# A SwiGLU whose turned results are copied out of their banks at the head of a gate group and split at its end

## The chip, the core and the metric

The kernel runs on one core of a Trainium2 chip. The metric is the device time of one execution in microseconds (us), the median of several runs; the profile is of one execution.

The engines are PE (matmul, with its weight load PEld), DVE (elementwise work on tensors), ACT (activations, copies and casts), POOL and SP (here they mostly issue DMAs). Results of PE land in PSUM, in eight banks of 128 x 512 float32; the other tiles lie in SBUF.

## What is computed

One layer of a decoder with 256 rows and a width of 2048: a combined projection, two kinds of attention, an output projection, a SwiGLU of inner width 5632 and a gated per-layer embedding, all in float32. What matters here is the SwiGLU:

```
f = rmsnorm(h, ffn_norm[i])
h = h + (jax.nn.silu(f @ w_gate[i]) * (f @ w_up[i])) @ w_down[i]
```

## The kernel before, in words

**Three products for one.** PE multiplies in a reduced float32 (type fp32r). To keep the precision, every operand is split in a high part (a cast to fp32r) and a low part (what the cast left out), and each product is made of three matmuls: high by high (line 400), the low part of the activations by the high part of the weights (401), and the high part of the activations by the low part of the weights (402). For each piece of a weight, ACT casts the high part (L352) from a raw tile that SP's DMA has filled, and DVE subtracts it from the raw tile to get the low part (L363). The parts lie in tiles called ringh and ringl, moreh and morel, and most. Some gate and up units are done by Strassen's scheme with seven products instead of eight: for those DVE also makes sums of the raw quarters (L362, L365, L366), and ACT and DVE hand pieces to each other.

**The order of the SwiGLU.** The inner width is cut in chunks of 1024 (the last has 512). The groups follow each other as g0, u0, g1, the first half of the down product of the chunk before, u1, its second half, g2 and so on. I call the down product that follows gate g1 "d1", and its halves the first and the second. The last chunk is one group for gate and up, gu5, and after it comes the last down product. Each group runs over units (one or two slices of 128 of the contracted dimension), and each unit over turns. In a turn, Python code emits casts and low parts of coming weights, then lets waiting side tasks do one step (`step`; a task says how many steps it wants to wait), then emits the matmuls. The engines take their instructions in the order in which they are emitted.

**The product that is turned.** When an up group ends, DVE multiplies its result with the silu of the gate into a tile called stage (L1012). The next group needs it turned, as the left operand of the down product: `ff_transpose` lets PE transpose it by blocks of 128 x 128 into four banks (L1032), four blocks in each, and `split_psum` makes the two parts from each bank: ACT casts the high part (L121) into ffTh, DVE subtracts (L122) into ffTl. All of this is emitted after the first product of the next gate group. The down product that reads ffTh and ffTl comes only after that gate group.

**What shares a tile.** Stage is one buffer. The end of a gate group (`gate_add`) takes it again: ACT copies the four gate banks into it (L997), POOL's DMA adds the Strassen sums U to it (L999), ACT applies silu (L1003), and the up group's end multiplies into it (L1012). Other work at these places: at the end of the Strassen units ACT copies a bank into U (L467) and DVE forms the sums there from the others (L468 to L471), which sets these banks free for the down product; at the end of a first down half ACT copies its four banks out (`add_later`, L915), and the up group that follows uses the same banks.

Of the kernel before, what the change touches and what calls it, by code (L numbers as in the profile page):

```python
# [8 lines left out]
F32 = mybir.dt.float32  # L9
# [4 lines left out]
ALU = mybir.AluOpType  # L14
# [21 lines left out]
def kernel(ctx, tc, x, p, positions, attn_norm, w_in, kv_norm, w_ukv, w_o, ffn_norm,  # L36
                             w_gate, w_up, w_down, ple_norm, w_ple_gate, w_ple_proj, final_norm,
                             inv_freq, out):
    nc = tc.nc
# [13 lines left out]
    def obank():  # L53
        b = B["rot"][B["next"] % len(B["rot"])]
        B["next"] += 1
        return b
# [62 lines left out]
    def split_psum(hi, lo, ps, scale=None):  # L119
        if scale is None:  # L120
            nc.scalar.copy(hi, ps)  # L121
            nc.vector.tensor_tensor(lo, ps, hi.bitcast(F32), op=ALU.subtract)  # L122
        else:
            nc.scalar.mul(hi, ps, scale)  # L124
            nc.vector.scalar_tensor_tensor(lo, ps, scale, hi.bitcast(F32), op0=ALU.mult, op1=ALU.subtract)
# [380 lines left out]
    def add(gen, wait=0, front=False):  # L506
        tasks.insert(0 if front else len(tasks), [wait, gen])
# [277 lines left out]
    def parts_tile(name, slot, shape=(8, SEQ)):  # L785
        return [big.tile([128, *shape], F32R, name=name + s, tag=f"{slot}{s}") for s in "hl"]
# [220 lines left out]
    def up_evac(ci, n, nb):  # L1007
        left = {"n": nb}

        def f(c, t, c0, c1, b, off=0):  # L1010
            st = S["ff"][:, t, c0 - off:c1 - off]
            nc.vector.scalar_tensor_tensor(st, b, S["rf"][:, t:t + 1], st, op0=ALU.mult, op1=ALU.mult)  # L1012
            left["n"] -= 1
            if left["n"] == 0:
                turned = ff_transpose(ci, n, S.pop("ff"))
                if ci < 5:
                    S["turned"] = turned
                else:
                    add(turned, 2)
        return f  # L1020

    def ff_transpose(ci, n, st):
        if ci == 5:
            ft = big.tile([128, 2, 6, SEQ], F32R, name="ffT", tag="att")
            tl = ffT[ci] = [ft[:, 0], ft[:, 1]]
        else:
            tl = ffT[ci] = parts_tile("ffT", "f0")
        for k in range(0, n // 128, 2):
            b = obank()
            for i in range(2):  # L1030
                for t in range(NT):
                    nc.tensor.transpose(b[:, (2 * i + t) * 128:(2 * i + t + 1) * 128],  # L1032
                                        st[:, t, (k + i) * 128:(k + i + 1) * 128], ident)
            split_psum(tl[0][:, k:k + 2, :], tl[1][:, k:k + 2, :], b.rearrange("q (a s) -> q a s", a=2))
            if k % 4 == 2:
                yield 1

    def ff_l(k, t):
        ci, kk = divmod(k, 8)
        return lhs_of(ffT[ci])(kk, t)  # L1040
# [224 lines left out]
    for k in range(2):  # L1265
        b = obank()
# [133 lines left out]
```

## Time and profile before

| | us |
|---|---|
| median of 3 runs | 1188.38 |
| range of the runs | 1187.52 to 1189.03 |
| the profiled execution | 1187.67 |
| its span, first to last instruction | 1185.9 |

In rows of the profile, a group names line, engine, operation, out<-in by tile names, the shape and a count. In rows of the timeline the first number is the start in us from the span's start, the second how long the row lasted; equal instructions that follow each other are one row with a count. In square brackets stands how long the engine was idle before the row and what ended that. Matmuls overlap, and their ends are modelled. "PEclk" is the clock that was granted to PE, as a share of the full one.

### The profile page before, as it was taken

The page shows a single profiled execution, that of the slowest core. Times are in us where ns is not written, and L with a number is a line of the kernel's source. Part 1 is how long each engine was busy: PE and PEld are TensorE (multiplying, and loading weights), DVE is VectorE, ACT ScalarE, POOL GpSimd, SP SyncE. Part 2 cuts the span into 40 slices and gives each one's busy share as a digit, 9 for nine tenths or more (in the row PEclk, how much of TensorE's full clock was granted, in tenths as well). Part 3 has the DMA queues.
Part 4 walks back from the last instruction along what each step waited for, and adds up shares of the span by engine and source line. Part 5 has one row for each costly group of instructions (what it writes and reads, how often), then busy time and mean ns, then how long its engine had stood idle before and what let it go on. Part 6 is the DMA issues. An engine that isn't in the chain of part 4 may idle for free.

```text
span 1185.9 us, 14606 instructions
## 1 busy us (share of the span) xinstructions
PE 1172.7 (99%) x5480; PEld 980.7 (83%) x5480; DVE 948.1 (80%) x1119; ACT 710.9 (60%) x908; POOL 57.3 (5%) x78
## 2 busy tenths in 40 slices
PE   9999999999999999999999999999999999999996
PEld 7888888899888888778888888888888888888886
DVE  5675756866567679998999899989998999897474
ACT  6735755456556754667657675658475756465453
POOL 5310000000000000000000000000000000000000
PEclk9999999999999999999999999999999999999999
DMA  9886877765584776596968697778768795846631
GB/s 303 288 341 213 293 270 264 261 213 200 200 335 141 284 250 229 202 310 173 339 218 301 178 332 227 274 209 326 238 216 262 268 279 198 329 145 220 202 107 72
DMA packets 87223, 287.80 MB, mean 243 GB/s; under 512 B 5676, under 2 KB 10080, under 8 KB 82544
## 3 DMA queue, kind: packets, MB, share of 16 engines
q1 hardware_dynamic: 77824, 240.15, 56.7%
q0 software_dynamic: 9040, 46.19, 14.2%
q8 instruction: 43, 0.70, 0.2%
q10 hardware_dynamic: 288, 0.52, 0.1%
q14 instruction: 28, 0.23, 0.1%
HBM read 252.24 MB, written 26.21 MB: 235 GB/s over the span
## 4 chain that ended last, share of the span: by engine, by line
PE 97%; DVE 1%; issue 1%; ACT 0%; POOL 0%; DVEq 0%; POOLq 0%
PE bank L402 31%; PE bank L400 31%; PE bank L401 31%; PE bank L138 1%; PE bank L593 1%; PE bank L1032 1%; PE bank L714 1%; PE bank L622 1%; DVE ringl L363 0%; PE bank L616 0%; PE bank L596 0%; PE bank L623 0%; PE bank L113 0%; DVE most L363 0%; DVE morel L363 0%
## 5 line engine op out<-in xcount | busy, mean ns | idle before, releaser
L352 ACT CAST ringh<-raw 128x1024 fp32r<-128x1024 f32 (+4 forms) x307 | 372.0, 1249 | 272.5 <-PE bank L401 113.6
L363 DVE TENSOR_TENSOR ringl<-raw,ringh 128x1024 fp32r<-128x1024 f32 (+4 forms) x307 | 443.4, 1467 | 105.8 <-ACT ringh L352 103.7
L400 PE MATMUL bank<-ringh,aT 128*128 128x512 f32 (+3 forms) x713 | 274.8, 385 | 0.0
L402 PE MATMUL bank<-ringl,aT 128*128 128x512 f32 (+3 forms) x713 | 270.6, 380 | 0.1
L401 PE MATMUL bank<-ringh,aT 128*128 128x512 f32 (+3 forms) x713 | 270.1, 379 | 0.0
L402 PEld LDWEIGHTS bank<-ringl,aT 128*128 128x128 f32 x713 | 133.9, 188 | 25.5 <-DVE ringl L363 1.3
L400 PEld LDWEIGHTS bank<-ringh,aT 128*128 128x128 f32 x713 | 134.1, 188 | 23.5 <-ACT aT L124 0.3
L401 PEld LDWEIGHTS bank<-ringh,aT 128*128 128x128 f32 x713 | 134.1, 188 | 23.4
L352 ACT CAST moreh<-raw 128x1024 fp32r<-128x1024 f32 (+2 forms) x70 | 79.8, 1174 | 19.4 <-DVE raw L362 9.2
L363 DVE TENSOR_TENSOR morel<-raw,moreh 128x1024 fp32r<-128x1024 f32 (+2 forms) x66 | 85.5, 1316 | 1.7 <-ACT moreh L352 1.2
L400 PE MATMUL bank<-ringh,ffTh 128*128 128x512 f32 x204 | 79.4, 389 | 0.0
L352 ACT CAST most<-raw 128x1024 fp32r<-128x1024 f32 (+2 forms) x58 | 56.8, 1006 | 37.7 <-DVE raw L362 14.4
L401 PE MATMUL bank<-ringh,ffTl 128*128 128x512 f32 x204 | 79.4, 389 | 0.0
L402 PE MATMUL bank<-ringl,ffTh 128*128 128x512 f32 x204 | 79.4, 389 | 0.0
L363 DVE TENSOR_TENSOR most<-raw,most 128x1024 fp32r<-128x1024 f32 (+2 forms) x58 | 66.3, 1163 | 1.6 <-ACT most L352 1.5
L362 DVE TENSOR_TENSOR raw<-raw 128x1024 f32<-128x1024 f32 x51 | 62.5, 1225 | 1.7
L402 PEld LDWEIGHTS bank<-ringl,ffTh 128*128 128x128 f32 x204 | 38.3, 188 | 8.0
L400 PEld LDWEIGHTS bank<-ringh,ffTh 128*128 128x128 f32 x204 | 38.3, 188 | 7.9
L401 PEld LDWEIGHTS bank<-ringh,ffTl 128*128 128x128 f32 x204 | 38.3, 188 | 7.9
L366 DVE TENSOR_TENSOR raw<-raw 128x512 f32<-128x512 f32 x51 | 35.3, 692 | 1.8
L365 DVE TENSOR_TENSOR raw<-raw 128x512 f32<-128x512 f32 x51 | 34.9, 684 | 0.0
L400 PE MATMUL bank<-most,aT 128*128 128x512 f32 x88 | 34.6, 393 | 0.0
(353 smaller groups left out, 1961.1 us busy)
## 6 DMA issues: line engine op xcount, KB each, us to landing
raw<-in_w_down SPq DMA_DIRECT2D x44, 1024.0 KB, 7.3
raw<-in_w_gate SPq DMA_DIRECT2D x35, 1024.0 KB, 7.6
raw<-in_w_up SPq DMA_DIRECT2D x32, 1024.0 KB, 7.6
raw<-in_w_in SPq DMA_DIRECT2D x40, 512.0 KB, 4.9
raw<-in_w_o SPq DMA_DIRECT2D x16, 1024.0 KB, 5.9
raw<-in_w_ple_gate SPq DMA_DIRECT2D x16, 1024.0 KB, 5.1
raw<-in_w_in SPq DMA_DIRECT2D x8, 1024.0 KB, 5.3
wsums<-in_w_up POOLq DMA_DIRECT2D x8, 1024.0 KB, 7.2
```

Source lines behind the costliest of these rows:

```text
L138: nc.tensor.transpose(b[:, (2 * i + t) * 128:(2 * i + t + 1) * 128], part[:, t, i * 128:(i + 1) * 128], ident)
L352: nc.scalar.copy(h[:, :, c0:c1], r[:, :, c0:c1])
L362: tt(f[:, 0:2], f[:, 1:2].to_broadcast([128, 2, 512]), f[:, 0:4:3], op=ALU.subtract)
L363: tt(l[:, :, c0:c1], r[:, :, c0:c1], h[:, :, c0:c1].bitcast(F32), op=ALU.subtract)
L365: tt(f[:, 3], f[:, 3], f[:, 0], op=ALU.subtract)
L366: tt(f[:, 2], f[:, 2], f[:, 3], op=ALU.subtract)
L400: nc.tensor.matmul(b, xh, h, start=start, stop=False)
L401: nc.tensor.matmul(b, xl, h, start=False, stop=False)
L402: nc.tensor.matmul(b, xh, l, start=False, stop=stop)
L593: nc.tensor.matmul(s[:, c0:c0 + nk], qT[:, q * 128:(q + 1) * 128], kT[:, 0:nk], start=True, stop=qpe is None)
L622: nc.tensor.matmul(o[:, 0:256], v(0), pT[:, 0:256], start=True, stop=False)
L714: nc.tensor.transpose(b[:, (2 * i + t) * 128:(2 * i + t + 1) * 128], src[:, t, col(i0 + i):col(i0 + i) + 128], ident)
```

## The change

For chunks 0 to 4, ACT no longer casts from the banks. It copies each turned bank, in float32, back into the place of stage that was just turned (L1040 of the changed kernel); the transposes themselves and their place are the same. A new task, `both_parts`, waits six steps, then emits one cast from stage to ffTh (L1047) in each of four steps, and then the four low parts from stage and ffTh (L1050): one, one, and the last two together. `front=True` puts the task ahead of others; as it is counted down in steps, it comes to stand in the last Strassen units and the last unit of the gate group. Chunk 5 is split as before.

```
         for k in range(0, n // 128, 2):
             b = obank()
...
-            split_psum(tl[0][:, k:k + 2, :], tl[1][:, k:k + 2, :], b.rearrange("q (a s) -> q a s", a=2))
+            h, l, f = tl[0][:, k:k + 2, :], tl[1][:, k:k + 2, :], b.rearrange("q (a s) -> q a s", a=2)
+            if ci == 5:
+                split_psum(h, l, f)
+            else:
+                kept = st[:, :, k * 128:(k + 2) * 128]
+                nc.scalar.copy(kept, f)
+                lows.append((l, kept, h))
             if k % 4 == 2:
                 yield 1
+
+        def both_parts():
+            for _, kept, h in lows:
+                nc.scalar.copy(h, kept)
+                yield 1
+            for i, (l, kept, h) in enumerate(lows):
+                nc.vector.tensor_tensor(l, kept, h.bitcast(F32), op=ALU.subtract)
+                if i < 2:
+                    yield 1
+        if lows:
+            add(both_parts(), 6, True)
```

Where this puts the instructions, on the engines that wait or are waited for. The rows are in the order in which an engine takes them; a minus is a row of the kernel before, a plus one of the changed kernel, and the number in a name such as raw_2917 tells buffers apart.

DVE at the head of g1, between the product of u0 and the first weights of the gate group:

```order
 L430 TENSOR_TENSOR U<-U,bank_80 128x512
 L1012 SCALAR_TENSOR_TENSOR stage<-U,rf,stage 128x512
-L122 TENSOR_TENSOR ffTl<-bank_77,ffTh 128x512
-L122 TENSOR_TENSOR ffTl<-bank_78,ffTh 128x512
-L122 TENSOR_TENSOR ffTl<-bank_79,ffTh 128x512
-L122 TENSOR_TENSOR ffTl<-bank_80,ffTh 128x512
 L363 TENSOR_TENSOR ringl<-raw_2917,ringh 128x1024 x2
 L363 TENSOR_TENSOR ringl<-raw_2919,ringh 128x1024
```

The four low parts are gone from here. On ACT, at the same place, four copies (L1040) stand where the four casts (L121) stood.

DVE at the end of g1 in the kernel before, from the last weights of the gate group to the first of d1:

```order
L363 TENSOR_TENSOR ringl<-raw_114,ringh 128x2048
L468 TENSOR_TENSOR U<-U,bank_80 128x512
L469 TENSOR_TENSOR U<-U,bank_78 128x512
L470 TENSOR_TENSOR U<-U,bank_79 128x512
L471 TENSOR_TENSOR U<-U,bank_79 128x512
L363 TENSOR_TENSOR morel<-raw_2917,moreh 128x2048
L363 TENSOR_TENSOR most<-raw_2919,most 128x2048
```

And the same place in the changed kernel:

```order
L363 TENSOR_TENSOR ringl<-raw_114,ringh 128x2048
L1050 TENSOR_TENSOR ffTl<-stage,ffTh 128x512 x2
L468 TENSOR_TENSOR U<-U,bank_80 128x512
L469 TENSOR_TENSOR U<-U,bank_78 128x512
L470 TENSOR_TENSOR U<-U,bank_79 128x512
L471 TENSOR_TENSOR U<-U,bank_79 128x512
L363 TENSOR_TENSOR morel<-raw_2917,moreh 128x2048
L1050 TENSOR_TENSOR ffTl<-stage,ffTh 128x512 x2
L363 TENSOR_TENSOR most<-raw_2919,most 128x2048
```

Two low parts now stand ahead of the sums of U, and two behind the first weights of d1.

ACT at the end of g1, with the engines whose semaphores an instruction waits for:

```order
+L1047 CAST ffTh<-stage 128x512
 L352 CAST ringh<-raw_113 128x1024 [waits DMAHW4_49,PE_49,Activation_49]
 L352 CAST ringh<-raw_113 128x1024 [waits PE_49,Activation_49]
+L1047 CAST ffTh<-stage 128x512
 L352 CAST ringh<-raw_114 128x2048 [waits DMAHW5_49,PE_49,Activation_49]
+L1047 CAST ffTh<-stage 128x512
 L467 COPY U<-bank_77 128x512 [waits PE_49]
 L352 CAST moreh<-raw_2917 128x2048 [waits DMAHW6_49,PE_49,Activation_49]
 L352 CAST most<-raw_2919 128x2048 [waits DMAHW7_49,DVE_49,PE_49]
-L997 COPY stage<-bank_83 128x512 [waits PE_49]
+L997 COPY stage<-bank_83 128x512 [waits DVE_49,PE_49,Activation_49]
 L997 COPY stage<-bank_84 128x512 [waits PE_49]
```

Three of the four casts are seen here (the first stands one row further up, ahead of another ringh cast). The first copy into stage, L997, has a new wait: for DVE's last low part, since that reads the stage tile which L997 writes. PE's order, and those of POOL and SP, stay as they were.

More of the change, by code (lines that the diff above doesn't have):

```diff
@@ L1027, in ff_transpose @@
             tl = ffT[ci] = parts_tile("ffT", "f0")
+        lows = []
         for k in range(0, n // 128, 2):
```

## The prediction

> **What bounds the kernel now.** First the page.
>
> ```profile
> PE 1172.7 (99%) x5480; PEld 980.7 (83%) x5480; DVE 948.1 (80%) x1119; ACT 710.9 (60%) x908; POOL 57.3 (5%) x78
> ```
>
> PE is the bound: its span is shortened only by a wait of PE that goes, and lengthened by every new one. So next the waits of PE, and their places in its timeline. Apart from its first instruction PE has, over the whole run, only two waits for another engine that reach 0.8 us, both in g1, the first gate group with the moved step at its head:
>
> ```profile
> 495.96 0.50 PE L402 MATMUL bank<-ringl,sumsmore_sums 128*128 128x512 f32 x1 [0.85 <-DVE ringl L363]
> ```
> ```profile
> 506.70 0.50 PE L402 MATMUL bank<-most,sumsmore_sums 128*128 128x512 f32 x1 [0.92 <-DVE most L363]
> ```
>
> Each waits for a low part that DVE had not finished. As a rule a matmul starts 0.23 us after the one before it, while its row lasts 0.39:
>
> ```profile
> 510.02 0.39 PE L401 MATMUL bank<-ringh,aT 128*128 128x512 f32 x1
> 510.25 0.50 PE L402 MATMUL bank<-ringl,aT 128*128 128x512 f32 x1
> ```
>
> So the idle of 0.85 and 0.92, with the 0.16 that two rows usually overlap, makes about 1.0 us for each stall. The windows view then shows why: between g1's head and 510.2 DVE does not pause, and the same holds in d1 (columns: stretch, its length, busy us of PE, PEld, DVE, ACT, POOL, then clock, DMA).
>
> ```profile
> 477.40:510.20 32.80, 31.03 (x136) 24.85 (x134) 32.45 (x34) 21.82 (x24) 0.00 (x0) 1.00 0.63 223
> ...
> 519.70:535.40 15.70, 15.70 (x71) 13.02 (x70) 15.48 (x16) 6.76 (x9) 0.00 (x0) 1.00 0.89 295
> ```
>
> **The head of a gate group.** Four copies take the place of four casts on ACT (L121 becomes L1040), and four low parts leave DVE. What that is worth depends on who waits for whom at g1's head:
>
> ```profile
> 474.31 2.06 ACT L121 CAST ffTh<-bank 128x512 fp32r<-128x512 f32 x4 [10.85 <-PE bank L1032]
> 476.23 1.08 ACT L352 CAST ringh<-raw 128x1024 fp32r<-128x1024 f32 x1
> ```
> ```profile
> 474.93 2.48 DVE L122 TENSOR_TENSOR ffTl<-bank,ffTh 128x512 fp32r<-128x512 f32 x4 [1.13 <-ACT ffTh L121]
> 477.34 1.23 DVE L363 TENSOR_TENSOR ringl<-raw,ringh 128x1024 fp32r<-128x1024 f32 x1
> ```
>
> DVE's first weight, ringl, starts at 477.34; the ringh that it needs ends at 476.23 + 1.08 = 477.31. So DVE does not start late because of its 2.48 us of low parts: it is held by ACT, whose four instructions stay where they were. In the new order DVE idles through these 2.48 us and starts ringl at the same moment. Gain of the head: 0, at best 0.1 us (ACT's casts beside DVE's reading were 0.03 us longer than its mean of 1.05). The two stalls stay, since DVE is full from there to the second.
>
> **The tail of g1, and d1.** Here the four casts and four low parts return. No row of before has these instructions, but the form from an SBUF tile is there:
>
> ```profile
> L122 DVE TENSOR_TENSOR aT<-stage,aT 128x512 fp32r<-128x512 f32 x7 | 4.8, 691 | 13.2 <-ACT aT L121 13.2
> ```
> ```profile
> L121 ACT CAST aT<-stage 128x512 fp32r<-128x512 f32 x7 | 4.4, 622 | 0.2
> ```
>
> Instructions in a row overlap by some 0.08 us on DVE and 0.1 on ACT (four took 2.48 and 2.06), so each low part adds 0.61 us and each cast 0.52. The ends: at least the 0.60 and 0.49 of the rows from a bank; at most the full 0.69 and 0.62.
>
> The Trainium skill, "VectorE: DVE Perf Modes" (the section on the TRN2 errata), has another rule: a VectorE operation pays a smaller fixed cost from SBUF (58 cycles) than from PSUM (120), so a moved low part would be 0.06 us cheaper than before. The trace does not bear it out: 691 ns from SBUF here, 2.48 us for four from the bank. By that rule the sum below would be about 1.3 us lower (an estimate from the page: 0.26 us in each of five groups).
>
> Now ACT, DVE and PE at this place.
>
> ```profile
> 505.62 4.76 ACT L352 CAST ringh<-raw 128x1024 fp32r<-128x1024 f32 x4 [0.88 <-DVE raw L366]
> 510.29 0.57 ACT L467 COPY U<-bank 128x512 f32<-128x512 f32 x1
> 510.76 1.92 ACT L352 CAST moreh<-raw 128x2048 fp32r<-128x2048 f32 x1
> 512.57 1.91 ACT L352 CAST most<-raw 128x2048 fp32r<-128x2048 f32 x1
> 514.38 2.03 ACT L997 COPY stage<-bank 128x512 f32<-128x512 f32 x4
> 516.29 1.94 ACT L352 CAST ringh<-raw 128x2048 fp32r<-128x2048 f32 x1
> ```
> ```profile
> 507.85 2.35 DVE L363 TENSOR_TENSOR ringl<-raw,ringh 128x1024 fp32r<-128x1024 f32 x2
> 510.42 2.29 DVE L363 TENSOR_TENSOR ringl<-raw,ringh 128x2048 fp32r<-128x2048 f32 x1 [0.22 <-ACT ringh L352]
> ...
> 514.67 0.68 DVE L471 TENSOR_TENSOR U<-U,bank 128x512 f32<-128x512 f32 x1
> 515.26 2.28 DVE L363 TENSOR_TENSOR morel<-raw,moreh 128x2048 fp32r<-128x2048 f32 x1
> 517.47 2.28 DVE L363 TENSOR_TENSOR most<-raw,most 128x2048 fp32r<-128x2048 f32 x1
> 519.67 2.28 DVE L363 TENSOR_TENSOR ringl<-raw,ringh 128x2048 fp32r<-128x2048 f32 x1
> ```
> ```profile
> 517.41 0.39 PE L400 MATMUL bank<-ringh,ffTh 128*128 128x512 f32 x1
> ```
> ```profile
> 536.45 0.39 PE L400 MATMUL bank<-ringh,aT 128*128 128x512 f32 x1
> ```
>
> Step by step. (1) The first cast lies in ACT's 0.88 us of idle before 505.62, free. The second delays the ringh pair of 506.6 by 0.52, of which 0.2 was spare: DVE's two ringl end at 510.5 instead of 510.2, and PE, which took the second one 0.05 us after its end, at 510.25 (above), is 0.3 late. (2) With the third cast the big ringh ends at 510.38 + 1.04 = 511.42, DVE's big ringl starts 1.0 later. Two low parts behind it: L468 to L471 are 2.25 late, L471 ends at 517.6. PE takes its bank at 517.41 + 0.3 = 517.7: just covered; with the dearer ends above PE would lose up to 0.4 here. (3) morel, then the last two low parts: the last one ends at about 521.0.
>
> (4) Here is the new wait. L997 copies the new gate results into the one stage buffer, which now still holds the old results, so its first copy waits for the last low part: 521.05 instead of 514.38, 6.7 us. ACT takes its instructions in order, so behind it stand three more L997, POOL's DMA that adds U to that tile, nine casts of raw weights and then L915, which empties the banks of d1. The ringh cast runs at 522.96 and takes 1.94, so DVE's ringl of 519.67 starts at 524.95, 5.3 late. From there to 535.4 DVE has 0.2 us of slack in 15.7 (the window above), and ACT follows it piece by piece:
>
> ```profile
> 533.09 1.06 ACT L352 CAST most<-raw 128x1024 fp32r<-128x1024 f32 x1 [0.85 <-DVE raw L366]
> 534.05 0.57 ACT L915 COPY copied<-bank 128x512 f32<-128x512 f32 x1
> ```
>
> (5) L915 of bank 0 starts at 534.05 + 5.3 = 539.35 and ends at 539.92. PE's first matmul of u1 writes that bank; it wants it at 536.45 + 0.3 = 536.75 and gets it at 539.97: a stall of 3.2 us. g1 with d1: 3.5 us. Through u1 DVE then runs 0.6 us later against PE than before; I take that as covered, and as up to 0.3 us per group if not.
>
> Loads: the step issues no DMA. SP's loads into tiles that the late low parts release go out up to 5.3 us later; a tile is read again some 20 us after it is freed, so I cost that at 0.
>
> **The other groups.** g4 is placed as g1: L915 and the matmul behind it lie alike.
>
> ```profile
> 904.66 0.58 ACT L915 COPY copied<-bank 128x512 f32<-128x512 f32 x1
> ```
> ```profile
> 907.08 0.39 PE L400 MATMUL bank<-ringh,aT 128*128 128x512 f32 x1
> ```
>
> So 3.5 again. In g2 DVE is further ahead and pauses before L915:
>
> ```profile
> 640.81 2.29 DVE L363 TENSOR_TENSOR ringl<-raw,ringh 128x2048 fp32r<-128x2048 f32 x1 [0.46 <-ACT ringh L352]
> ```
> ```profile
> 654.92 1.22 DVE L363 TENSOR_TENSOR most<-raw,most 128x1024 fp32r<-128x1024 f32 x1 [0.77 <-ACT most L352]
> ```
> ```profile
> 656.06 0.59 ACT L915 COPY copied<-bank 128x512 f32<-128x512 f32 x1 [0.22 <-PE bank L402]
> ```
> ```profile
> 659.94 0.39 PE L400 MATMUL bank<-ringh,aT 128*128 128x512 f32 x1
> ```
>
> The ringl of 640.81 moves by 4.9 (the same wait), the pause takes up 0.8 to 0.9: L915 at 660.1, done at 660.7, PE wants bank 0 at 659.94: 0.8 us. g3 I take as g2. The last group, gu5, has no L997; there the DVE chain itself goes to the SwiGLU's last product (L1012), which PE turns next:
>
> ```profile
> 1017.55 0.75 DVE L1012 SCALAR_TENSOR_TENSOR stage<-U,rf,stage 128x512 f32<-128x512 f32 x1 [0.20 <-ACT stage L991]
> ```
> ```profile
> 1019.86 0.38 PE L1032 MATMUL bank<-ident,stage 128*128 128x128 f32 x2
> ```
>
> It ends at 1018.30 + 1.0 + 4 x 0.61 = 1021.8; PE's second turn, 0.1 after 1019.86 and 0.3 late, wanted it at 1020.3: 1.5, with the 0.3 of step (1) 1.8 us. Sum: 3.5 + 0.8 + 0.8 + 3.5 + 1.8 = 10.4 us. The profiled execution took 1187.67 (span 1185.9 and 1.8 around it), so 1198.1; it lies 0.7 under the median of 1188.38, so 1198.8 for the median.
>
> **The rivals.** *Only the near stalls* (slower, small): DVE or ACT makes up the 5.3 us before L915, and only 4 x 0.3 and gu5's 1.8 less 0.3 remain, 2.7 us: 1191.1. It needs 3.5 us of slack in 519.7 to 535.4, where the window shows 0.2. *Faster*: the 2.48 us taken from DVE's head let it start ringl early, both 1.0 us stalls and the three or so short ones of 0.1 at the gates' ends go, and the tail stays under cover: 1188.38 - 2.4 = 1186.0. For it speaks that DVE is full for 33 us after the head. It decides at the end of the first ringh: it would have to come about 2 us before 477.31, and the last low part before 517, not 521. *The clock*: a stall over 3 us might cost PE its rate. The run's first matmuls go at 0.42 us instead of 0.23:
>
> ```profile
> 5.04 1.69 PE L113 MATMUL bank<-junk 128*128 128x512 bf16 x4
> ```
>
> That lasted at least this row's 1.7 us and at most the 6.7 from the span's start to its end; half of it was lost, 0.8 to 3.4, in the middle 2.1. After each of the two stalls of 3.2 us that makes 4.2 more: 1203.0. Against it: the stalls of 1.0 us left the granted clock at 1.00. The Trainium skill, "TensorE: Matmul & The Clock Gate", Part 1, says that the clock halves after an idle window of about 3.4 us, which is just longer than the stall; no run here shows which.
>
> **How the numbers follow.** Forecast 0.76, near stalls only 0.09, clock 0.08, faster 0.05, and 0.02 that everything stays hidden at 1188. The forecast's own range: below, casts that fall into ACT's idle (0.5 in each of five groups, -2.5); above, the full durations (0.6 a group, +3.0) and 0.3 for each up group (+1.2): 1196.3 to 1203.0. The range reaches down for the case of near stalls in part and up into the clock's case: 1193.0 to 1203.5. A difference under 0.2%, 2.4 us, cannot be told from none. Faster by more than that 0.04, within it 0.07 (half of the near stalls' case, the rest of the faster one, the hidden one), slower 0.89.
>
> **What would show it.** Right: ringl at g1's head still starts with the end of ringh; the first L997 of g1 starts with the end of DVE's last L1050, about 6.7 us later against the gate's last matmul; PE waits for L915 at the heads of u1 and u4 for about 3 us, of u2 and u3 for under 1, and for L1012 in gu5. Wrong: the two stalls of g1 gone, or no wait of PE for L915.

## The result, and the profile after

The changed kernel takes 1202.54 us (median of 5 runs, 1200.41 to 1202.88), the kernel before 1188.38 us: a ratio of 1.0112, with a 95% interval of 1.0097 to 1.0126. It is slower, by 14.2 us where 10.4 were forecast; the time lies in the range of the prediction, near its upper end. The profiled execution took 1202.54 us, its span is 1200.8 us.

The engines' busy times on the page:

```profile
PE 1178.4 (98%) x5480; PEld 982.0 (82%) x5480; DVE 949.0 (79%) x1119; ACT 720.7 (60%) x928; POOL 55.8 (5%) x78
```

PE runs the same 5480 matmuls and is busy for 5.7 us more, in a span that is 14.9 us longer. The waits of PE (who waited for whom: us in total, times, the longest):

```profile
PE bank L400 <- ACT copied L915: 7.4, 4, 3.0
PE bank L113 <- DVE junk L108: 2.0, 1, 2.0
PE bank L1033 <- DVE stage L1012: 1.3, 1, 1.3
PE bank L402 <- DVE ringl L363: 1.2, 3, 0.8
PE bank L402 <- DVE most L363: 0.9, 1, 0.9
```

The four waits for L915 and the one for L1012 are new, and so are two short ones for ringl; the two of 0.8 and 0.9 are still there. The wait for L108 is that of PE's first instruction, the same in every kernel. At g1's head, DVE's first ringl is held by ACT's ringh as before, now after 3.53 us of idle:

```profile
477.68 2.36 DVE L363 TENSOR_TENSOR ringl<-raw,ringh 128x1024 fp32r<-128x1024 f32 x2 [3.53 <-ACT ringh L352]
```

At g1's tail the timelines of DVE and of ACT show the chain that ends at L915:

```profile
520.05 1.29 DVE L1050 TENSOR_TENSOR ffTl<-stage,ffTh 128x512 fp32r<-128x512 f32 x2
521.25 2.29 DVE L363 TENSOR_TENSOR most<-raw,most 128x2048 fp32r<-128x2048 f32 x1
525.34 3.43 DVE L363 TENSOR_TENSOR ringl<-raw,ringh 128x2048 fp32r<-128x2048 f32 x2 [1.80 <-ACT ringh L352]
```
```profile
521.45 2.06 ACT L997 COPY stage<-bank 128x512 f32<-128x512 f32 x4 [5.07 <-DVE ffTl L1050]
523.36 3.41 ACT L352 CAST ringh<-raw 128x2048 fp32r<-128x2048 f32 x3
...
539.72 2.04 ACT L915 COPY copied<-bank 128x512 f32<-128x512 f32 x4
```

The last low part ends at 520.05 + 1.29 = 521.34, L997 starts behind it, the ringh cast behind that, and DVE, done with most at 523.54, idles 1.80 us for it. PE's first matmul of u1 follows the copy of bank 0. Then comes what the likeliest case did not hold:

```profile
540.35 0.79 PE L400 MATMUL bank<-ringh,aT 128*128 128x512 f32 x1 [2.94 <-ACT copied L915]
540.94 0.63 PE L401 MATMUL bank<-ringh,aT 128*128 128x512 f32 x1
541.37 0.63 PE L402 MATMUL bank<-ringl,aT 128*128 128x512 f32 x1
```
```profile
540.30:546.50 6.20, 6.15 (x15) 4.86 (x16) 4.46 (x6) 6.05 (x8) 1.11 (x1) 0.51 0.70 202
```

The matmuls go 0.43 us apart instead of 0.23, and the windows view shows the granted clock at 0.51 for 6 us. After the wait in u4, which is as long, they don't:

```profile
919.57 0.50 PE L400 MATMUL bank<-ringh,aT 128*128 128x512 f32 x1 [2.97 <-ACT copied L915]
919.91 0.39 PE L401 MATMUL bank<-ringh,aT 128*128 128x512 f32 x1
```

PE's order is the same in both kernels, so the n-th matmul of one trace can be set against the n-th of the other. Where the distance between them grows:

| place | forecast, us | measured, us |
|---|---|---|
| first 7 us of the run | | 0.35 |
| g1: head, and the two stalls in it | 0 | 0.0 |
| end of g1 | 0.3 | 0.33 |
| u1, wait for L915 | 3.2 | 3.22 |
| u1, matmuls at half rate | only as a rival | 2.91 |
| u2, u3 | 0.8 + 0.8 | 1.03 + 0.99 |
| end of g4, u4's wait | 0.3 + 3.2 | 0.34 + 3.35 |
| later in u4 | | 0.31 |
| gu5 | 1.8 | 1.96 |
| small ones | | 0.07 |
| sum | 10.4 | 14.86 |

The 0.35 us at the start have nothing to do with the change: in the trace before, the full clock is granted from 6.38 us on, here from 7.05, and 0.67 us more at half rate cost 0.34.

### The profile page after: what moved, and what is told of

Same layout as the page of the kernel before. It is cut to its first block, busy times and chain, and to the rows that moved or that the text cites. A ratio compares the mean times of both kernels' runs of the same rounds, so it can differ in the third digit from the quotient of the medians.

```text
span 1200.8 us, 14625 instructions
## 1 busy us (share of the span) xinstructions
PE 1178.4 (98%) x5480; PEld 982.0 (82%) x5480; DVE 949.0 (79%) x1119; ACT 720.7 (60%) x928; POOL 55.8 (5%) x78
## 4 chain that ended last, share of the span: by engine, by line
PE 85%; DVE 7%; ACT 4%; issue 3%; DMA 1%; ACTq 0%; DVEq 0%; POOL 0%; POOLq 0%
PE bank L400 26%; PE bank L402 26%; PE bank L401 26%; ACT ringh L352 2%; DVE ringl L363 1%; DVE morel L363 1%; PE bank L138 1%; DVE raw L362 1%; PE bank L593 1%; DVE ffTl L1050 1%; PE bank L1033 1%; DMA raw<-in_w_down 1%; DVE raw L366 1%; PE bank L714 1%; PE bank L622 1%
```

## The experiments

Theory A is the chain of the prediction: at the tails DVE's added load and the wait of L997 in ACT's queue make PE wait; the head gives nothing, as ACT's ringh holds DVE there. Against it stand: the wait alone, the load alone, and a cost that has nothing to do with the head. Each edit below is made to the changed kernel, unless the text says that it is made to the kernel before.

**The wait of L997, taken out of the way.** Only the place of the four copies L997 (and of the DMA and the silu behind them) is changed; they are given out by a task in the next step, so they stand behind the ringh cast.

```
-        nc.scalar.copy(S["ff"][:, t, c0:c1], b)
+        S.setdefault("out", []).append((t, c0, c1, b))
         if (c, t) == (1, 1):
...
+            add(copies(S.pop("out"), S["U"]))
```

> The copies of the gate's banks (L997) are given out one step later, so that they stand behind the ringh cast of the first down half in ACT's order and no longer hold it up; the casts and low parts stay at the end of the gate group. Theory A (ACT's queue and DVE's load together): DVE's big ringl of d1 then starts when DVE's most ends, at about 523.5 instead of 525.3 us, so 1.8 of the 5.3 us go and 3.5 stay: PE waits for L915 about 1.3 us at the heads of u1 and u4 instead of 3.1, not at all at u2 and u3, the clock stays full: 1202.5 - 2.9 - 3.6 - 1.8 = about 1194 us. Rival B (the wait in the queue is all): no wait for L915 at all, 1202.5 - 2.9 - 6.5 - 1.8 = about 1191 us. Rival C (DVE's load is all): as the changed kernel, 1200 to 1202.5 us.

Measured: 1194.07 us (1193.36 to 1194.98), ratio 1.0048 (1.0035 to 1.0060). DVE goes from most to ringl without a pause, and PE's first wait in u1 is 1.05 us:

```profile
521.56 2.29 DVE L363 TENSOR_TENSOR most<-raw,most 128x2048 fp32r<-128x2048 f32 x1
523.76 3.42 DVE L363 TENSOR_TENSOR ringl<-raw,ringh 128x2048 fp32r<-128x2048 f32 x2
```
```profile
538.77 0.50 PE L400 MATMUL bank<-ringh,aT 128*128 128x512 f32 x1 [1.05 <-ACT copied L915]
539.10 0.39 PE L401 MATMUL bank<-ringh,aT 128*128 128x512 f32 x1
```

Theory A, to 0.1 us. The queue's wait was 1.8 of the 5.3 us by which the chain of d1 was late; 3.5 are DVE's own load and the casts.

**The clock.** Twelve matmuls of data at hand, into a bank that is free at that time, ahead of u1 and of u4. Their result is not used.

```
+            if i > wide and u.name in ("u1", "u4") and u.idx == n == 0:
+                for _ in range(12):
+                    nc.tensor.matmul(B["acc"][3], aT[0][:, 0, 0:128], aT[0][:, 0:2, :], start=True, stop=True)
```

> Twelve matmuls of data that lies there, into a bank that is free, are put ahead of the first matmul of u1 and of u4 (2.7 us of PE's time; their result is overwritten). Theory A (the idle of 3 us lets the clock fall): the wait for L915 remains as long as it was, counted with the added matmuls, but no matmul after it goes at half rate: 1202.5 - 2.9 = about 1199.6 us, granted clock 0.997 or more. Rival (the slow matmuls at the head of u1 have another cause, at that place): they stay slow, 1202.5 us or more.

Measured: 1199.99 us (1199.87 to 1200.23), ratio 1.0097 (1.0081 to 1.0112), mean clock 0.998 where the changed kernel had 0.995. The matmuls behind the added ones go at full rate:

```profile
537.74 2.88 PE L1382 MATMUL bank<-aT 128*128 128x512 f32 x12
540.88 0.50 PE L400 MATMUL bank<-ringh,aT 128*128 128x512 f32 x1 [0.26 <-ACT copied L915]
541.22 0.39 PE L401 MATMUL bank<-ringh,aT 128*128 128x512 f32 x1
```

PE waits for L915 as before, busy with nothing of use, and the half rate is gone, 2.55 us by the medians: the idle of 3 us is what lowered the clock.

**The head, freed.** One line moves in the main loop:

```
+            high_parts(late)
             if "mid" in S and not u.strassen and u.mixed and 2 * u.idx + n >= 0 and len([*S["mid"]]) >= 0:
                 S.pop("mid")
-            high_parts(late)
```

> At the head of a gate group ACT casts the ringh of the coming weights ahead of the four copies L1040, in its idle time. Theory A (DVE at the head was held by ACT's ringh, and DVE is full from there): DVE's first ringl of g1 starts when L1012 ends, about 474.2 instead of 477.7 us; the two stalls of 1.0 us in g1 go (-2.1), DVE arrives at the end of g1 some 1 us earlier against PE, the wait at u1 falls from 3.1 to about 2 and the clock stays full (-2.9 - 1.1): about 1196 us. Rival (the head has no worth, something else sets the two stalls): both stalls stay, 1199.6 to 1202.5 us.

Measured: 1189.13 us (1188.50 to 1191.27), ratio 1.0009 (1.0001 to 1.0018). DVE starts its weights as soon as the product of u0 is done, 3.5 us earlier against PE, and in PE's waits both stalls of g1 are gone:

```profile
473.58 0.75 DVE L1012 SCALAR_TENSOR_TENSOR stage<-U,rf,stage 128x512 f32<-128x512 f32 x1
474.25 3.49 DVE L363 TENSOR_TENSOR ringl<-raw,ringh 128x1024 fp32r<-128x1024 f32 x3
```
```profile
PE bank L400 <- ACT copied L915: 3.3, 2, 2.3
PE bank L113 <- DVE junk L108: 2.0, 1, 2.0
```

Right in kind, too small by 7 us in size: I forecast 1196. The lead of DVE also removed the waits in u2 and u3, two thirds of that in u4, and all of gu5's, which I had not counted. The wait of 2.3 us left in u1 is followed by the full rate in the trace. Two of the eleven runs, 1191.21 and 1191.27, have a mean clock of 0.996 where the other nine have 0.997 and at most 1189.34 us; a fall of the clock there is likely, but these runs have no trace.

**Only the first product.** `if ci == 5` becomes `if ci`, so that only the product turned in g1 is split late.

> Only the product turned at the head of g1 is copied and split late; the later ones are split at the head as before. Theory A (the groups' terms add up): g1 and u1 alone cost 0.3 + 3.2, and 2.9 more if the clock falls there: 1188.4 + 3.5 = about 1192 us, or 1195 with the clock's part. Rival (the loss is one of the whole chain, a delay that is handed from group to group): well over 1195 us, or nearly nothing.

Measured: 1194.23 us (1192.01 to 1195.92), ratio 1.0048 (1.0036 to 1.0061). In its trace PE has this one new wait of 3 us, followed by half rate:

```profile
540.61 0.80 PE L400 MATMUL bank<-ringh,aT 128*128 128x512 f32 x1 [2.97 <-ACT copied L915]
541.20 0.63 PE L401 MATMUL bank<-ringh,aT 128*128 128x512 f32 x1
```
```profile
540.60:546.60 6.00, 5.99 (x14) 4.76 (x15) 4.30 (x5) 5.98 (x8) 1.11 (x1) 0.51 0.71 195
```

Behind u1 the distance to the kernel before stays as it is, so the delay of one group is not handed on to the next. The runs spread over 3.9 us; the one of 1192.01 has a mean clock of 0.997, the profiled one of 1194.69 has 0.995. But a run of 1194.19 has 0.997 too, so the clock alone does not explain the spread.

**The early ringh alone.** The same moved line in the kernel before.

> The kernel before, with nothing changed but that ACT casts the ringh of the coming weights ahead of the four casts L121 at a gate group's head. Theory A (there DVE's four low parts still stand ahead of its ringl, so that the early ringh frees nothing): ringl of g1 still starts at about 477.3 us, both stalls of 1.0 us stay, 1188.1 us. Rival (the gain of the third experiment came from the early ringh alone, not from the low parts that were moved away): the two stalls go, about 1186 us.

Measured: 1189.12 us (1188.07 to 1190.35), ratio 1.0010 (1.0001 to 1.0019). DVE's low parts fill the time in which ringl could now have started, and a stall of 0.84 is still there:

```profile
475.67 2.48 DVE L122 TENSOR_TENSOR ffTl<-bank,ffTh 128x512 fp32r<-128x512 f32 x4 [1.12 <-ACT ffTh L121]
478.07 1.21 DVE L363 TENSOR_TENSOR ringl<-raw,ringh 128x1024 fp32r<-128x1024 f32 x1
```
```profile
496.67 0.50 PE L402 MATMUL bank<-ringl,sumsmore_sums 128*128 128x512 f32 x1 [0.84 <-DVE ringl L363]
```

The 0.1% more lies in g4 and gu5, 0.5 and 0.3 us by the matmuls; the cause stays open. So neither edit alone frees DVE at the head: with the low parts moved, ringh holds it; with ringh early, the low parts do.

**Both, and L997 later.**

> The changed kernel with both edits of the first and third experiment: ringh ahead of the copies at the head, L997 behind the ringh cast at the tail. Theory A (what was left in the third, 2.5 us at u1 and 1.1 at u4, holds 1.8 us of the queue's wait each): 0.7 at u1, none at u4, so 1189.1 - 1.8 - 1.1 = about 1186.2 us, less than the kernel before. Rival (with DVE ahead, the load of the low parts alone makes these waits): as the third, 1189 us.

Measured: 1185.99 us (1185.21 to 1186.61), ratio 0.9983 (0.9974 to 0.9991): faster than both kernels, by 0.17% against the one before, where the prediction took 0.2% as the least that can be told from none. Of PE's waits in the SwiGLU only one is left:

```profile
PE bank L113 <- DVE junk L108: 2.0, 1, 2.0
PE bank L400 <- ACT copied L915: 0.4, 1, 0.4
```

**The low parts on POOL.** `nc.vector.tensor_tensor(l, ...)` becomes `nc.gpsimd.tensor_tensor(l, ...)` in `both_parts`.

> The changed kernel, but the four low parts (L1050) are made by POOL instead of DVE; copies, casts and the order are the same. Theory A (DVE's 2.4 us and the wait for them are the loss): the low parts end before ACT reaches L997 (516.4), DVE is only as late as the four casts make it, about 1 us; the stalls of 0.3 at the gates' ends stay, none for L915: about 1189 us. Rival (POOL is slow, or its work slows DVE): a low part takes 3 us or DVE's rows grow longer, the waits move to them, over 1192 us.

Measured: 1205.29 us (1204.25 to 1205.85), ratio 1.0144 (1.0130 to 1.0158). The low parts do end early, the last of g1 at 513.85, but DVE's subtractions beside them take nearly twice as long. DVE's rows of g1's end in this kernel, then the group of all ringl of this shape here, and the same group of the changed kernel:

```profile
508.17 8.97 DVE L363 TENSOR_TENSOR ringl<-raw,ringh 128x1024 fp32r<-128x1024 f32 x4
```
```profile
L363 DVE TENSOR_TENSOR ringl<-raw,ringh 128x1024 fp32r<-128x1024 f32 x159 | 208.1, 1337 | 34.6 <-ACT ringh L352 32.9
```
```profile
L363 DVE TENSOR_TENSOR ringl<-raw,ringh 128x1024 fp32r<-128x1024 f32 x159 | 190.0, 1221 | 27.7 <-ACT ringh L352 25.5
```

The waits of PE moved there:

```profile
PE bank L402 <- DVE ringl L363: 9.3, 12, 1.3
PE bank L402 <- DVE most L363: 2.0, 1, 2.0
```

No wait for L915 is left, as theory A says, but the price is higher. The rival was right, by its second half. Part of the price is the clock: in g1, g4 and gu5 it falls to half for 3.41 us each, from 509.24, 891.53 and 1021.24, which costs up to half of that, 1.7 us, a time, at most 5.1 of the 18.0 us by which this trace is longer than that of the kernel before.

**POOL, with the head freed.**

> The low parts on POOL, and ringh ahead of the copies at the head. Theory A: both stalls of g1 go and no wait for L915 is left, 1188.1 - 2.1 - 0.3 = about 1185.7 us. Rival (POOL slow or in DVE's way): over 1188 us.

Measured: 1193.06 us (1192.58 to 1193.31), ratio 1.0042 (1.0029 to 1.0055). The rival again: both stalls of g1 go, but in g1, g4 and gu5 PE waits for ringl at the end of the gate group. In g1 the clock falls to half for 3.41 us, behind two such waits of 0.57 and 1.27 us.

```profile
PE bank L402 <- DVE ringl L363: 4.8, 5, 1.3
```

**The low parts in the first half of the group.** `add(both_parts(), 6, True)` becomes `add(both_parts(), 0, True)`.

> The changed kernel with a wait of 0 instead of 6: casts and low parts are given out in the first half of the gate group, the last two low parts ahead of the most that PE waits for at 506.7. Theory A (DVE is full from g1's head to its end, so low parts cost 0.6 us each there too, but no longer the wait of L997): the second stall of g1 grows from 1.0 to about 3.4 us, nothing is late at the end of g1 and no wait for L915 is left in u1 to u4; g4 and gu5, where DVE is nearly full, lose 0 to 2 us each: about 1188 + 2.4 + 2 = 1192 us, from 1190.5 to 1195. Rival (the low parts find gaps there): 1188 us or less.

Measured: 1199.96 us (1197.90 to 1202.08), ratio 1.0100 (1.0086 to 1.0113). The mechanism holds, the size does not. There is no wait for L915; PE waits for weights instead, 2.4 us at the longest:

```profile
PE bank L402 <- DVE ringl L363: 5.8, 3, 2.4
PE bank L402 <- DVE most L363: 2.6, 2, 2.4
```

Set against the kernel before, matmul by matmul, g1 loses 2.9 us, and g4 and gu5 2.5 each, where I had 0 to 2. Behind the waits of g4 and gu5 PE goes at half rate again, which I had not counted at all, and loses 1.4 and 1.7 us more:

```profile
883.34 0.79 PE L402 MATMUL bank<-ringl,sumsmore_sums 128*128 128x512 f32 x1 [2.37 <-DVE ringl L363]
883.93 0.63 PE L400 MATMUL bank<-ringh,sumsmore_sums 128*128 128x512 f32 x1
```

**The same, with the head freed.**

> The same wait of 0, and ringh ahead of the copies at the head. Theory A (the head then gives DVE 3.5 us, the low parts take 2.4 back in the same group, 1.1 us stay): of the two stalls of 1.0 us about half goes, nothing is late at the tails: about 1187 us. Rival (the gain of the third experiment needs the low parts at the end): 1189 us or more.

Measured: 1186.89 us (1186.27 to 1187.67), ratio 0.9990 (0.9981 to 0.9999). As forecast: the first stall goes, the second stays, at 1.4 us, and nothing is late at the tails.

```profile
PE bank L402 <- DVE most L363: 1.4, 1, 1.4
```

## Why the prediction was right, and where not

**The head** was right. With the 0.35 us by which the whole second trace lies later, ringl starts at 477.68 - 0.35 = 477.33, forecast 477.34, and both stalls stay. The freed head and the early ringh alone show why: two things held DVE there, and the change removes one of them.

**The tail** was right step by step. Less 0.35, the last low part ends at 520.99 (forecast 521.0), L997 starts at 521.10 (521.05), ringl at 524.99 (524.95) and L915 at 539.37 (539.35). The stall of 0.3 at the gate's end is there as well, and PE does not wait for the bank of L471.

**What the wait of L997 is worth** reads wrongly in step (4). The prediction put the 5.3 us of delay behind "the new wait". The run with L997 out of the way shows that only 1.8 of them come from it; with the casts' 1.0 and four low parts of 0.61, 3.4 in all, DVE's rows end about 3.5 us late without it. A wait that ends last isn't the whole of a delay: the next releaser was 1.8 us behind it.

**The other groups**: right, and a little small, 1.03 and 0.99 against 0.8, 1.96 against 1.8. About 0.1 us of each is the start after a stall: the first matmul takes 0.50 and the next comes 0.34 behind it instead of 0.23. I had put the low parts' load in u1 to u4 at nothing or 0.3 per group; 0.31 came in u4, nothing in the others.

**The step that failed is the clock.** I gave the rival 0.08, since stalls of 1.0 us had left the clock at 1.00, and put it after both long stalls at 2.1 each. It came after one of the two in the profiled execution, at 2.91, and the fall of the mean clock, to 0.995 or 0.996 from 0.998, is in all five runs: the likeliest case, without it, lies 1.6 us under the fastest of them. The difference of the forecast to the median, 3.7 us, is this 2.9 and 1.2 in the other terms, less the 0.4 by which the two profiled executions lay differently at the run's start and to their medians (0.35 - 0.71): 2.9 + 1.2 - 0.4 = 3.7. The bounds of the clock's price, 0.8 to 3.4 us, held it. The two runs with a mean clock of 0.996 took 1.7 to 2.5 us less than the three with 0.995.

The reason given against this rival, that stalls of 1.0 us had left the clock at 1.00, was too far from the case: by the traces in the last section, the idle that counts is that within one step of 3.413 us, 0.91 at such a stall and 2.12 in u1. That the time lies in the range is in part luck. The wait in u4 missed the half rate by where it lay on these steps; with a second fall the time would have been about 1205.4 (an estimate: 1202.54 + 2.9), above the range. The time also lies in the likeliest case's own range, up to 1203.0, but the room of 4.2 us there was meant for dearer rows and for the up groups; all terms but the clock took 1.2 of it, and the clock's 2.9 filled the rest.

**A slip in the sum of a rival.** The near stalls are priced with 0.3 in four groups besides gu5's 1.5, while the sum of the forecast has 0.3 in g1, g4 and gu5 alone. By its own terms that rival is 3 x 0.3 + 1.5 = 2.4 us, so 1190.8 and not 1191.1. It changes nothing in the account.

The faster case, 1186.0, failed for the reason that was given: ringl did not come earlier. Where it does, with L997 out of the way as well, the time is 1185.99. That the two numbers agree so closely is chance: beside that run the kernel before took 1187.92, so the gain was 1.9 us where the case had 2.4.

## What to carry to other kernels

Before costing work that is taken from an engine, look at what the next instruction on that engine waits for besides: if another engine holds it to the same moment, the removal gives nothing until that is moved too, and both edits together may pay where each alone costs or does nothing. Work that is moved to the end of a stage is paid there in full if the engine is full; its cost is then read from the first PE row that the chain reaches. And for a stall of PE of 2 to 3 us, or several short ones close together, count with a second cost of 1.4 to 2.9 us, since the clock may fall. Whether it does depends on where the stall lies, and that differs from run to run. Filling the stalls with matmuls of no use saved 2.55 us here.

## What the runs showed of the hardware

**The clock after an idle PE.** Idle of 2.94 us was followed by half rate, with matmuls 0.43 us apart for 5.7 us; idle of 2.97 in the same execution was not, and idle of 2.37 was, in another kernel. So the length alone does not decide. Where the stall lies does. The traces record when the granted clock changes, and within each of the twelve traces all these changes lie whole multiples of 3.413 us apart. In the changed kernel the full clock begins at 7.05, the half at 539.53, 156 such steps later, and the full one again at 546.35, two steps on. The rows show the step ahead of that fall, the stretch at half rate, and the two steps over which the wait of u4 lies (columns as in the prediction, the granted clock third from the end):

```profile
536.11:539.52 3.41, 1.30 (x6) 0.75 (x4) 3.38 (x5) 1.80 (x2) 0.00 (x0) 1.00 0.68 269
539.53:546.35 6.82, 6.00 (x14) 4.74 (x15) 5.09 (x6) 6.79 (x10) 1.11 (x1) 0.50 0.61 180
```
```profile
914.99:918.40 3.41, 1.61 (x8) 0.99 (x6) 3.38 (x5) 1.46 (x2) 0.00 (x0) 1.00 0.75 303
918.41:921.82 3.41, 2.25 (x10) 1.87 (x11) 1.85 (x2) 3.41 (x7) 0.46 (x1) 1.00 0.26 44
```

PE stood idle for 2.12 us of the first step, while the end of a step cut the wait of u4 in 1.81 and 1.16. From 10 to 1150 us the twelve traces have eight falls, each behind a step with 1.82 to 2.12 us of idle; no other step reaches 1.82 but one of 1.86, from 507.39 in the run with the low parts early, which was not followed by half rate. So in these traces the bound lies at 1.8 to 1.9 us, no closer, since the ends of matmuls are modelled. The half rate lasted one step where the next one had at most 0.5 us of idle, and two where it had 0.82 and 0.99 (u1, in the changed kernel and with only the first product moved). Where the steps lie differs from run to run: the full clock began between 5.6 and 7.9 us in the twelve traces. The Trainium skill, "TensorE: Matmul & The Clock Gate", Part 1, has the clock watched in windows of about 3.4 us that run freely; the steps of 3.413 us agree with that. By the same part of the Trainium skill the clock falls after at least one idle window; here a little over half a window of idle was enough.

**POOL beside DVE.** A 128x1024 subtraction of DVE takes 1.22 us alone. Of the four ringl at g1's end in the run with POOL, the three of this shape take 2.31, 2.30 and 2.32 us, 1.1 more each; the last, 128x2048, has no low part beside it and takes its usual 2.28. One pair of rows:

```profile
510.20 1.42 POOL L1050 TENSOR_TENSOR ffTl<-stage,ffTh 128x512 fp32r<-128x512 f32 x1 [0.80 <-ACT ffTh L1047]
```
```profile
510.40 2.30 DVE L363 TENSOR_TENSOR ringl<-raw,ringh 128x1024 fp32r<-128x1024 f32 x1
```

DVE's row starts behind POOL's and ends 1.08 us after POOL's end (512.70 and 511.62). At all four low parts of g1 it is 1.08 or 1.09, little less than the whole 1.22, as if DVE's row stood still for as long as POOL's ran. The Trainium skill, "GPSIMD Engine Reference", 1. Specifications, says that GpSimd shares its way into SBUF with VectorE, for DVE instructions with two SBUF inputs; this trace agrees.

**Source of the operand.** The low part from SBUF took 685 ns here, from the bank 684 before:

```profile
L1050 DVE TENSOR_TENSOR ffTl<-stage,ffTh 128x512 fp32r<-128x512 f32 x20 | 12.9, 685 | 0.0
```
```profile
L122 DVE TENSOR_TENSOR ffTl<-bank,ffTh 128x512 fp32r<-128x512 f32 x20 | 12.4, 684 | 9.4 <-ACT ffTh L121 9.4
```

So the rule of the Trainium skill, "VectorE: DVE Perf Modes" (the section on the TRN2 errata), that the prediction weighed would have been wrong for this form by its 0.06 us.
